# An encoder layer on one core: the first projections from an x that comes transposed, the norm as side work, the recurrences moved behind the first attention heads

## The chip, the cores and the metric

The kernel runs on one core of one Trainium2 chip. The metric is the device time of one execution in microseconds (us), as the median of the runs; lower is better. The engines are named as in the profile: PE is TensorE, DVE VectorE, ACT ScalarE, POOL GpSimd, SP SyncE. Each takes its own instructions in a fixed order, and an instruction that waits holds up all behind it on its engine.

## The reference

One layer with S = 256 tokens of D = 1024. The normed x goes through one wide matrix, whose columns feed four mixers; their outputs are gated, projected and added, and a feed-forward part and a gated embedding follow.

```python
xn = _rms_norm(x, norm1_g[i])
(a_x, a_g, b_q, b_k, b_v, c_q, c_kv, c_kpe,
 d_q, d_k, d_v, d_g, gate_logits) = jnp.split(xn @ w_in[i], IN_OFFSETS, axis=-1)
y_a = _rglru_mixer(a_x, a_g, conv_w[i], conv_b[i], lru_wa[i], lru_ba[i], lru_wx[i], lru_bx[i],
                   lru_lambda[i])
...
y_b = _diff_attention(b_q, b_k, b_v, diff_q_g[i], diff_k_g[i], diff_lam[i], diff_sub_g[i],
                      lam_init, cos_b, sin_b)
y_c = _mla(c_q, c_kv, c_kpe, mla_qa_g[i], mla_wuq[i], mla_kva_g[i], mla_wukv[i],
           mla_q_g[i], mla_k_g[i], cos_c, sin_c)
y_d = _retention(d_q, d_k, d_v, d_g, ret_gn_g[i], cos_d, sin_d)
gates = jax.nn.sigmoid(gate_logits.reshape(b, s, N_BRANCH, D_MODEL) + gate_b[i])
...
x = x + merged @ w_out[i]
h = _rms_norm(x, norm2_g[i])
x = x + jnp.square(jax.nn.relu(h @ w_ff1[i])) @ w_ff2[i]
ple_gate = jax.nn.sigmoid(_rms_norm(x, norm3_g[i]) @ w_ple_gate[i])
x = x + ple_gate * (p[i] @ w_ple_proj[i])
```

`_rglru_mixer` is a convolution over tokens, two gated linear recurrences (one in each direction) and a gelu gate; the other three are kinds of attention. The norm multiplies each token by one factor (over its 1024 values) and each column by a gain. A token's factor is the same for all columns, so it can be applied to a projection's rows afterwards as well.

## The kernel before, in words

**Weights.** All matrices are packed in one array in the order of their use. `load` (L364) brings up to 512 rows by 512 columns, 1 MB, into one of three `raw` buffers, by a DMA on SP's queue; an issue for a buffer that is not free waits, and so do the DMAs behind it. `pieces` (L374) turns 1024 columns of `raw` into two reduced-precision tiles: `hi`, a rounded copy (by ACT, or by DVE for every second piece from the eighth), and `lo`, the difference, always by DVE. There are five buffers for each (`NR`). The activations are split in the same way (`xTh`, `xTl`, by `split_scaled`, L223), and a product is three matmuls: hi with high, lo with high, hi with low. All of them go through the helper line L199.

**Two shapes of projection.** `a_mode` (L396) has the tokens in the output's rows: per 128 rows of weights six matmuls of 512 columns, into two PSUM banks. `b_mode` (L434) has the output's columns in rows: 48 matmuls of 256 columns per 256 columns of weights, into one bank. There are four such banks ("acc") and four for all else ("mm").

**Side work.** The element-wise parts are Python generators in the list `side`. After each load's worth of matmuls `tick` (L339) lets the first four of the list go on by a step each until a credit is used up; `finish` (L352) runs one to its end. A scheduler then sets the order of the instructions of each engine by priorities (`high_priority`): the pieces stand 60 instructions ahead of their place.

**The start.** x comes in rows (four DMAs, L231), then the column parameters (L232); ACT squares and sums x, DVE scales it by the tokens' factors (L457), 16 PE transposes and eight `split_scaled` give `xTh`, `xTl`. Then:

- four times `a_in(u)` (L506): a `b_mode` projection and a convolution (`xc`); each starts `a_mix(u)`: loads `bd` (block-diagonal gate matrices, L525), matmuls of `xc` with `bd`, sigmoids, exp, tanh, square and square root, then two scans on DVE, one per direction;
- `b_in(c)` for c = 0, 1: q, k, v of four heads each (`a_mode`), with side work `b_rot` (norm per head, rotation, transposes) and `b_mix` (scores, softmax);
- four times `a_out(u)` (L563), which finishes `a_mix(u)`, projects the gate, takes its gelu (`gel`) and multiplies; then `c_in` (the latents; 384 and 320 columns), the gates and the merges.

ACT keeps its functions in tables, and an ACT_TABLE_LOAD stands in its order where the next function is in another one: the sigmoids, the exponentials and tanh, the square roots and the gelu are in different ones here.

## Time and profile before

| | |
|---|---|
| median of 3 runs | 734.09 us (733.2 to 734.31) |
| the profiled execution | 732.92 us |
| its span, first to last instruction | 731.1 us |
| PE busy | 714.7 us, 98% of the span |
| DVE busy | 526.2 us, 72% |
| ACT busy | 427.7 us, 58% |
| POOL busy | 49.3 us, 7% |
| first instruction of PE | 7.51 us after the span's start |
| DMA | 128.47 MB, mean 176 GB/s |

The times of the trace count from the span's start. A group's row gives its source line, engine, operation, output and inputs, shapes and count, then its busy time, the mean duration of one in ns, and the idle time of the engine ahead of it with what ended it. Matmuls start closer together than they last (0.12 us apart at 0.28 us each, for 256 columns), so PE's pace is read from the starts. A full-precision (f32) matmul shows as two records.

### The profile page before, as it was taken

How to read it: one execution, taken by the hardware profiler on the slowest of the kernel's cores; microseconds unless marked ns; L12 is line 12 of the kernel's file. 1: busy time of each engine (PE TensorE's matmuls, PEld its weight loads, DVE VectorE, ACT ScalarE, POOL GpSimd, SP SyncE). 2: the span in 40 equal slices, each digit the busy share in tenths (PEclk: the TensorE clock that was granted, in tenths of full speed). 3: DMA queues.
4: the chain of work that ended last, by engine and by line, in shares of the span. 5: the costliest groups of instructions: out<-in, count | busy, mean ns of one | idle time of the engine just before them, and what ended most of it. 6: DMA issues, size and time to landing. Idle time of an engine off the chain costs nothing.

```text
span 731.1 us, 10616 instructions
## 1 busy us (share of the span) xinstructions
PE 714.7 (98%) x4066; PEld 622.6 (85%) x4066; DVE 526.2 (72%) x893; ACT 427.7 (58%) x744; POOL 49.3 (7%) x58
## 2 busy tenths in 40 slices
PE   5999999999999999999999999999999999999997
PEld 4988889997888898888888888878899999888886
DVE  5988978998777879976775788576666666446652
ACT  7589867483755996556654443545755555445551
POOL 0000012222011033110000101000000000000000
PEclk9999999999999999999999999999999999999999
DMA  8754544365344254444545475553565555636611
GB/s 312 260 212 173 172 173 145 114 248 182 134 162 137 91 177 169 173 159 144 179 166 217 138 256 197 191 184 143 177 225 176 173 177 185 215 118 229 233 53 58
DMA packets 22802, 128.47 MB, mean 176 GB/s; under 512 B 2656, under 2 KB 2912, under 8 KB 9440
## 3 DMA queue, kind: packets, MB, share of 16 engines
q1 hardware_dynamic: 22752, 127.80, 49.8%
q8 instruction: 32, 0.52, 0.3%
q14 instruction: 18, 0.15, 0.1%
HBM read 126.74 MB, written 1.05 MB: 175 GB/s over the span
## 4 chain that ended last, share of the span: by engine, by line
PE 64%; DVE 1%; ACT 0%; issue 0%
PE acc L199 57%; PE mm L199 3%; PE mm L212 2%; PE mm L203 1%; ACT hi L196 0%; DVE lo L190 0%; DVE gate L193 0%; DVE pg L190 0%; DVE y L193 0%; DVE xs L190 0%; ACT pg L196 0%
## 5 line engine op out<-in xcount | busy, mean ns | idle before, releaser
L190 DVE TENSOR_TENSOR lo<-raw,hi 128x1024 fp32r<-128x1024 f32 (+3 forms) x226 | 268.2, 1192 | 116.6 <-ACT hi L196 116.0
L196 ACT ACTIVATE hi<-raw 128x1024 fp32r<-128x1024 f32 (+2 forms) x200 | 207.7, 1043 | 192.6 <-PE acc L199 161.2
L199 PE MATMUL acc<-hi,xTh 128*128 128x512 f32 (+3 forms) x376 | 146.3, 389 | 0.0
L199 PE MATMUL acc<-hi,xTl 128*128 128x512 f32 (+3 forms) x376 | 142.8, 380 | 0.0
L199 PE MATMUL acc<-lo,xTh 128*128 128x512 f32 (+3 forms) x376 | 142.5, 379 | 0.0
L199 PE MATMUL acc<-hi,y 128*128 128x512 f32 x448 | 142.1, 393 | 0.0
L199 PE MATMUL acc<-xTl,hi 128*128 128x256 f32 x384 | 109.2, 285 | 0.2 <-DVE xTl L193 0.2
L199 PE MATMUL acc<-xTh,hi 128*128 128x256 f32 x384 | 109.2, 286 | 0.0
L199 PE MATMUL acc<-xTh,lo 128*128 128x256 f32 x384 | 108.7, 284 | 0.0
L199 PEld LDWEIGHTS acc<-hi,y 128*128 128x128 f32 x448 | 84.1, 188 | 17.5
L199 PE MATMUL acc<-lo,y 128*128 128x512 f32 x224 | 87.8, 392 | 0.0
L199 PEld LDWEIGHTS acc<-hi,xTl 128*128 128x128 f32 x376 | 70.6, 188 | 13.2
L199 PEld LDWEIGHTS acc<-hi,xTh 128*128 128x128 f32 x376 | 70.7, 188 | 12.9
L199 PEld LDWEIGHTS acc<-lo,xTh 128*128 128x128 f32 x376 | 70.8, 188 | 12.2
L199 PEld LDWEIGHTS acc<-xTl,hi 128*128 128x128 f32 x384 | 74.1, 193 | 0.7 <-DVE xTl L193 0.6
L199 PEld LDWEIGHTS acc<-xTh,hi 128*128 128x128 f32 x384 | 73.9, 193 | 0.1
L199 PEld LDWEIGHTS acc<-xTh,lo 128*128 128x128 f32 x384 | 73.8, 193 | 0.1
L199 PEld LDWEIGHTS acc<-lo,y 128*128 128x128 f32 x224 | 42.1, 188 | 8.3
L199 PE MATMUL acc<-hi,h 128*128 128x512 f32 x128 | 40.8, 398 | 0.0
L199 PEld LDWEIGHTS acc<-hi,h 128*128 128x128 f32 x128 | 24.0, 188 | 5.7
L199 PE MATMUL acc<-lo,h 128*128 128x512 f32 x64 | 25.3, 396 | 0.0
L199 PE MATMUL acc<-hi,cT 128*128 128x384 f32 (+1 forms) x80 | 24.2, 369 | 0.8 <-ACT cqp L196 0.8
(225 smaller groups left out, 889.9 us busy)
## 6 DMA issues: line engine op xcount, KB each, us to landing
raw<-in_weights_dram SPq DMA_DIRECT2D x104, 1024.0 KB, 4.8
raw<-in_weights_dram SPq DMA_DIRECT2D x6, 512.0 KB, 3.5
raw<-in_weights_dram SPq DMA_DIRECT2D x4, 576.0 KB, 3.8
bd<-in_lru_dram SPq DMA_DIRECT2D x8, 256.0 KB, 5.3
gb<-in_gate_b_dram SPq DMA_DIRECT2D x8, 256.0 KB, 5.2
dec<-in_decay_dram SPq DMA_DIRECT2D x8, 256.0 KB, 6.2
raw<-in_weights_dram SPq DMA_DIRECT2D x2, 768.0 KB, 4.3
raw<-in_weights_dram SPq DMA_DIRECT2D x2, 640.0 KB, 3.7
```

The lines of the kernel that those rows point to most:

```text
L190: nc.vector.tensor_tensor(out=o, in0=x, in1=y, op=op)
L196: nc.scalar.activation(o, x, f, **kw)
L199: nc.tensor.matmul(o, lhsT=lhsT, rhs=rhs, start=start, stop=stop)
L203: nc.tensor.matmul(o, lhsT=lhsT, rhs=rhs, start=start, stop=stop, skip_group_check=True)
L212: nc.tensor.transpose(o, x, ident[:x.shape[0], :x.shape[0]])
```

## The change

The inputs have a further array, `xT`, which is x with its columns in rows. The first projections are now q, k and v of heads 0 to 3, with x without the tokens' factors: `x1` is `xT` times the gain, split in hi and lo. The evacuations of these projections multiply by the factors `r1`, which `norm1`, a side generator, works out meanwhile from x in rows. `norm1` also makes the derived parameters, spreads the factors along columns by two matmuls, multiplies `xT` by them on POOL (`x1r`), and splits that into `xTh`, `xTl` for all later projections; the transposes are gone. The first weights come in three parts on SP's queue, between those of `xT`; the column parameters come on ACT's queue. The first four pieces have 512 columns in place of 1024, and the first two of their `hi` are DVE's. Twelve matmuls of zeros (`cold`) stand first on PE. The four `a_in` follow, and each `a_mix` is put ahead of the attention's generators in `side`.

```diff
+    raw0 = raws.tile([P, 2048], F32, tag="raw", name="raw", bufs=3)
     with tc.high_priority(FIRST):
-        for t in range(2):
-            for c in range(2):
-                w = slice(512 * c, 512 * c + 512)
-                nc.sync.dma_start(xs[:, t, w], a['x'][0, t * P:(t + 1) * P, w])
-        nc.sync.dma_start(par[:, :O_LATE], a['params'][:, :O_LATE])
+        nc.scalar.dma_start(par[:, :8], a['params'][:, :8])
+        nc.scalar.dma_start(par[:, 8:O_LATE], a['params'][:, 8:O_LATE])
+
+        cold = small.tile([P, P], F32, tag="cold", name="cold", bufs=1)
+        nc.vector.memset(cold, 0.0)
+        pt = mm_bank()
+        for _ in range(WARM):
+            mm(pt[:, 0:P], cold, cold, True, True)
...
-            if count[0] % 2 == 0 and count[0] in V_HI:
+            if count[0] <= 2 or count[0] % 2 == 0 and count[0] - 2 in V_HI:
...
-            for p0 in range(0, kc, 2):
-                kp = min(2, kc - p0)
+            fine = 1 if count[0] < 4 else 2
+            for p0 in range(0, kc, fine):
+                kp = min(fine, kc - p0)
...
-        with tc.high_priority(FIRST):
-            for t in range(2):
-                r_ = rstd(xs[:, t, :], lambda: SH("xsq"))
-                nc.vector.tensor_scalar(out=xs[:, t, :], in0=xs[:, t, :], scalar1=r_, scalar2=None, op0=MULT)
-            for k2 in range(4):
...
-                        transpose(pt[:, k, t * P:(t + 1) * P], xs[:, t, kk * P:(kk + 1) * P])
...
+        def norm1():
+
             for t in range(2):
+                for c in range(2):
+                    w = slice(512 * c, 512 * c + 512)
+                    nc.sync.dma_start(xs[:, t, w], a['x'][0, t * P:(t + 1) * P, w])
+            nc.sync.dma_start(par[:, O_LATE:], a['params'][:, O_LATE:])
+            yield 2.0
+            for t in range(2):
+                r1.append(rstd(xs[:, t, :], lambda: SH("xsq"), 'rst1'))
+                yield 1.5
+            derived_params()
+            yield 3.0
+
+            pt = mm_bank()[:, :S]
+            for t in range(2):
+                mm(pt[:, t * P:(t + 1) * P], r1[t].to_broadcast([P, P]), ident, True, True)
+            rows = SH("rows")[:, :S]
+            act(rows, pt, AF.Copy)
+            yield 0.5
+            for j in range(2):
+                nc.gpsimd.tensor_tensor(out=x1r[j], in0=x1r[j], in1=rows.unsqueeze(1).to_broadcast([P, 4, S]), op=MULT)
+                yield 0.3
+            for k in range(8):
+                split_scaled(xTh[:, k, :], xTl[:, k, :], x1r[k // 4][:, k % 4, :], c1('norm1_g', k))
...
+                if pre is not None:
+                    while len(r1) < 2:
+                        next(pre)
+                kw = [{} if pre is None else dict(scale=r1[t]) for t in range(2)]
...
-                        act(x[:, t, :], ps[t][:, 256 * p:256 * p + 256], AF.Copy)
+                        act(z[:, t, :], ps[t][:, 256 * p:256 * p + 256], AF.Copy, **kw[t])
...
+            nc.sync.dma_start(x1r[0][:, 0:2], a['xT'][:, 0:2])
+            nc.sync.dma_start(raw0[:, 0:512], src[:, 0:512])
+            nc.sync.dma_start(raw0[:, 512:1024], src[:, 512:1024])
+            nc.sync.dma_start(x1r[0][:, 2:4], a['xT'][:, 2:4])
+            nc.sync.dma_start(raw0[:, 1024:2048], src[:, 1024:2048])
+            nc.sync.dma_start(x1r[1], a['xT'][:, 4:8])
...
+        pre = start(norm1())
+        for p, (r0, qT, rq, rk, kT, _, v) in enumerate(b_in(0, (x1k(0), x1k(1)), pre)):
+            gb.append(start(b_mix(p, qT, rq, kT, v, yb), (r0, rk)))
+        finish(pre)
         for u in range(4):
             xc = a_in(u)
-            if u == 0:
-                derived_params()
             ha.append(L("rr").rearrange("p (f s) -> p f s", s=S))
             ga.append(start(a_mix(u, xc, ha[u])))
-        yb = yhl()
-        for c in range(2):
-            for p, (r0, qT, rq, r1, kT, _, v) in enumerate(b_in(c)):
-                gb.append(start(b_mix(2 * c + p, qT, rq, kT, v, yb), (r0, r1)))
+
+            side.insert(u, side.pop())
+        for p, (r0, qT, rq, rk, kT, _, v) in enumerate(b_in(1)):
+            gb.append(start(b_mix(2 + p, qT, rq, kT, v, yb), (r0, rk)))
```

**Where the instructions move.** First, ACT's first work before; `xsq` are the squares of x, `nst` the sums and factors.

```order
L196 ACT_TABLE_LOAD
L196 ACTIVATE eps<-eps 128x1
L196 ACTIVATE xsq,nst<-xs 128x512 x3
L196 ACTIVATE nst<-nst,eps 128x1
L196 ACTIVATE xsq,nst<-xs 128x512
L196 ACTIVATE nst<-nst,eps 128x1
L196 ACTIVATE xTh<-mm,par 128x256
L196 ACTIVATE hi<-raw 128x1024
```

And in the change, from the third row on; the y tiles at the top hold x1 and xT.

```order
L199 ACTIVATE y_119<-y_123,par 128x256 x4
L199 ACTIVATE hi<-raw 128x512 x2
L199 ACTIVATE y_121<-y_124,par 128x256 x4
L199 ACTIVATE hi<-raw 128x1024 x4
L199 ACTIVATE xsq,nst<-xs 128x512 x4
L199 ACTIVATE nst<-nst,eps 128x1 x2
L199 ACTIVATE bx<-acc,nst 128x256 x4
L199 ACTIVATE spt<-par 128x16
L199 ACT_TABLE_LOAD
L199 ACTIVATE spt<-spt 128x16
L199 ACTIVATE lams<-lams 128x2
L199 ACTIVATE hi<-raw 128x1024
```

The squares, the factors, the first evacuations (`bx`) and the start of the derived parameters now stand between the hi of the eighth piece and that of the ninth.

Second, SP's queue ahead of the bd matrices of the second recurrence (u = 1; bd_409 and bd_411), before:

```order
L371 DMA raw_424<-in_weights_dram 128x2048
L371 DMA raw_524<-in_weights_dram 128x2048
L371 DMA raw_594<-in_weights_dram 128x2048
L371 DMA raw_660<-in_weights_dram 128x2048
L525 DMA bd_409<-in_lru_dram 128x512
L525 DMA bd_411<-in_lru_dram 128x512
```

And in the change, where they are bd_728 and bd_730:

```order
L379 DMA raw_757<-in_weights_dram 128x2048
L379 DMA raw_853<-in_weights_dram 128x2048
L379 DMA raw_923<-in_weights_dram 128x2048
L379 DMA raw_989<-in_weights_dram 128x2048
L379 DMA raw_1036<-in_weights_dram 128x2048
L551 DMA bd_728<-in_lru_dram 128x512
L551 DMA bd_730<-in_lru_dram 128x512
```

raw_757 is the fourth recurrence projection's load, raw_853 and raw_923 are those of q in `b_in(1)`, raw_989 and raw_1036 those of k. PE uses bd_728 directly behind the fourth recurrence projection:

```order
L202 MATMUL acc_756<-xTh_114,lo_788 128x256
L202 MATMUL mm_817<-xc_476,bd_627 128x256 x2
L202 MATMUL mm_822<-xc_476,bd_627 128x256 x2
L202 MATMUL mm_828<-xc_565,bd_728 128x256 x2
L202 MATMUL mm_833<-xc_565,bd_728 128x256 x2
L202 MATMUL acc_851<-hi_855,xTh_114 128x512
L202 MATMUL acc_851<-lo_856,xTh_114 128x512
```

raw_1036 takes the buffer of raw_853, which is free when lo of its second piece (piece 24, lo_872) is made.

Third, ACT from the first gelu of `a_out` on, before:

```order
L196 ACT_TABLE_LOAD
L196 ACTIVATE gel<-acc 128x512
L196 ACTIVATE y_1181<-gel 128x512
L196 ACTIVATE hi<-raw 128x768
L196 ACTIVATE gel<-acc 128x512
L196 ACTIVATE y_1181<-gel 128x512
L196 ACTIVATE bsq<-bx 128x512
L196 ACTIVATE hi<-raw 128x768
```

And in the change, from the same gelu; the row ahead of these is the last of four sigmoids that read the matmuls with bd_919:

```order
L199 ACT_TABLE_LOAD
L199 ACTIVATE gel<-acc 128x512
L199 ACT_TABLE_LOAD
L199 ACTIVATE aa<-rr,sp 128x256
L199 ACTIVATE y_1183<-gel 128x512
L199 ACTIVATE rr<-rr,sp 128x256
L199 ACTIVATE aa<-rr,sp 128x256
L199 ACTIVATE hi<-raw 128x768
L199 ACTIVATE rr<-rr,sp 128x256
L199 ACTIVATE sq<-aa 128x512
L199 ACT_TABLE_LOAD
L199 ACTIVATE gel<-acc 128x512
```

The next hi of 768 columns (the third piece of `c_in`) stands 24 rows further down, behind five more table loads, four sigmoids, the third gelu and the last square roots. `aa` and `rr` are the recurrences' exponentials and tanh. DVE's way to the lo of that piece in the change, from the last squares on:

```order
L196 SCALAR_TENSOR_TENSOR rr<-sq,rr 128x512
L582 MEMSET aa 128x2
L687 TENSOR_REDUCE bsm<-mm 128x2 x2
L193 TENSOR_TENSOR bsm<-bsm,brs 128x2
L193 TENSOR_TENSOR ii<-ii,rr 128x512 x2
L586 SCALAR_TENSOR_TENSOR rr<-aa,ii 128x512 x2
L653 TENSOR_REDUCE brs<-bsq 128x8
L193 TENSOR_TENSOR rr<-rr 128x512
L193 TENSOR_TENSOR lo<-raw,hi 128x768
```

Row six (L586) is two scans. Over the whole program ACT has 24 table loads in its order, 18 before.

More of the change, by code (lines that the diff above doesn't have):

```diff
@@ L28 @@
 V_HI = range(8, 60)
+WARM = 12
 O_AX, O_AG, O_BQ, O_BK, O_BV = 0, 1024, 2048, 3072, 4096
@@ L160, in _pack @@
     import numpy as np
-    return {'x': np.asarray(w['x']), 'weights': _pack_weights(w), 'params': _pack_params(w), 'lru': _pack_lru(w),
+    return {'x': np.asarray(w['x']),
+            'xT': np.ascontiguousarray(np.asarray(w['x'])[0].T.reshape(8, P, S).transpose(1, 0, 2)), 'weights': _pack_weights(w), 'params': _pack_params(w), 'lru': _pack_lru(w),
             'pT': np.ascontiguousarray(np.asarray(w['p'])[0, 0].T.reshape(2, P, S).transpose(1, 0, 2)),
@@ L238, in encoder_kernel @@
         nc.vector.memset(eps[:, j:j + 1], v)
-    act(eps[:, 2:3], eps[:, 0:1], AF.Sqrt)
     nhalf = const.tile([P, 16], F32, name="nhalf")
@@ L255, in derived_params @@
     def derived_params():
-        nc.sync.dma_start(par[:, O_LATE:], a['params'][:, O_LATE:])
         gr = par[:, O_GR:O_LAM].rearrange("p (j c w) -> p j c w", j=2, c=2)
@@ L303, in encoder_kernel, with rstd @@
     xTl = near.tile([P, 8, S], F32R, name="xTl")
-    def rstd(src, scratch):
-        st = small.tile([P, 2], F32, tag="nst", name="nst")
+    def rstd(src, scratch, tag="nst"):
+        st = small.tile([P, 2], F32, tag=tag, name="nst", bufs=4 if tag == "nst" else 2)
         sq = scratch()
@@ L452, in SH @@
             return br.tile([P, 512], F32, tag="SH", name=name, bufs=NS)
-        with tc.high_priority(FIRST):
+        r1 = []
+        done = set()
+        def norm1():
             for t in range(2):
-                r_ = rstd(xs[:, t, :], lambda: SH("xsq"))
-                nc.vector.tensor_scalar(out=xs[:, t, :], in0=xs[:, t, :], scalar1=r_, scalar2=None, op0=MULT)
-            for k2 in range(4):
-                pt = mm_bank().rearrange("p (k s) -> p k s", s=S)
-                for t in range(2):
-                    for k in range(2):
-                        kk = 2 * k2 + k
-                        transpose(pt[:, k, t * P:(t + 1) * P], xs[:, t, kk * P:(kk + 1) * P])
-                for k in range(2):
-                    kk = 2 * k2 + k
-                    split_scaled(xTh[:, kk, :], xTl[:, kk, :], pt[:, k, :], c1('norm1_g', kk))
+                for c in range(2):
[19 more added lines that the diff above has]
+                split_scaled(xTh[:, k, :], xTl[:, k, :], x1r[k // 4][:, k % 4, :], c1('norm1_g', k))
+                if k % 2:
+                    yield 1.0
         def y4():
@@ L613, in b_in @@
                         ss = small.tile([P, 2, 4], F32, tag="brs", name="brs", bufs=8)
-                        pairs[p] += [start(b_rot(j, x, dst, ss)), dst, ss]
+                        pairs[p] += [start(b_rot(j, z, dst, ss), () if pre is None else (pre,)), dst, ss]
                     else:
-                        pairs[p].append(x)
+                        pairs[p].append(z)
             return pairs
@@ L945, in encoder_kernel, with x1k, get @@
         ha, ga, gb, gc = [], [], [], []
+        x1 = yhl()
+        early[W_in, 0, O_BQ] = raw0
+        x1r = [y4().bitcast(F32) for _ in range(2)]
+        with tc.high_priority(FIRST):
+            o = offs[W_in, 0, O_BQ][0]
+            src = a['weights'][o:o + 512 * 512].rearrange("(p c) -> p c", c=2048)
+            nc.sync.dma_start(x1r[0][:, 0:2], a['xT'][:, 0:2])
[4 more added lines that the diff above has]
+            nc.sync.dma_start(x1r[1], a['xT'][:, 4:8])
+            act(eps[:, 2:3], eps[:, 0:1], AF.Sqrt)
+        def x1k(i):
+            def get(k):
+                if k not in done:
+                    done.add(k)
+                    with tc.high_priority(FIRST if k == 0 else AHEAD_S + 20):
+                        split_scaled(x1[k // 4][0][:, k % 4, :], x1[k // 4][1][:, k % 4, :], x1r[k // 4][:, k % 4, :],
+                                     c1('norm1_g', k))
+                return x1[k // 4][i][:, k % 4, :]
+            return get
+        yb = yhl()
+        pre = start(norm1())
+        for p, (r0, qT, rq, rk, kT, _, v) in enumerate(b_in(0, (x1k(0), x1k(1)), pre)):
+            gb.append(start(b_mix(p, qT, rq, kT, v, yb), (r0, rk)))
+        finish(pre)
         for u in range(4):
             xc = a_in(u)
-            if u == 0:
-                derived_params()
             ha.append(L("rr").rearrange("p (f s) -> p f s", s=S))
             ga.append(start(a_mix(u, xc, ha[u])))
-        yb = yhl()
-        for c in range(2):
-            for p, (r0, qT, rq, r1, kT, _, v) in enumerate(b_in(c)):
-                gb.append(start(b_mix(2 * c + p, qT, rq, kT, v, yb), (r0, r1)))
+            side.insert(u, side.pop())
+        for p, (r0, qT, rq, rk, kT, _, v) in enumerate(b_in(1)):
+            gb.append(start(b_mix(2 + p, qT, rq, kT, v, yb), (r0, rk)))
         pace[0] = G1
```

9 lines of the change are left out of this document (6 added, 3 removed).

## The prediction

> **What bounds the kernel now.** I read the page first, then the waits of TensorE.
>
> ```profile
> PE 714.7 (98%) x4066; PEld 622.6 (85%) x4066; DVE 526.2 (72%) x893; ACT 427.7 (58%) x744; POOL 49.3 (7%) x58
> ...
> bd<-in_lru_dram SPq DMA_DIRECT2D x8, 256.0 KB, 5.3
> ```
>
> ```profile
> PE mm L212 <- DVE nst L190: 7.5, 1, 7.5
> ```
>
> TensorE (PE) is busy for 98% of the span; of its 16.4 us without work 7.5 lie ahead of its first instruction. So a change is worth what it does to the start, less what it makes PE wait for later. The timeline of PE shows that the start costs more than those 7.5 us.
>
> ```profile
> 7.51 0.66 PE L212 MATMUL mm<-ident,xs 128*128 128x128 f32 x2 [7.51 <-DVE nst L190]
> ...
> 11.74 0.56 PE L199 MATMUL acc<-xTh,hi 128*128 128x256 f32 x1
> ...
> 13.32 0.41 PE L199 MATMUL acc<-xTh,hi 128*128 128x256 f32 x1
> 13.54 0.35 PE L199 MATMUL acc<-xTl,hi 128*128 128x256 f32 x1
> ...
> 16.73 0.28 PE L199 MATMUL acc<-xTl,hi 128*128 128x256 f32 x1
> 16.85 0.28 PE L199 MATMUL acc<-xTh,lo 128*128 128x256 f32 x1
> ```
>
> ```profile
> 30.77 1.89 PE L199 MATMUL mm<-xc,bd 128*128 128x256 f32 x8
> ```
>
> ```profile
> 45.59 0.39 PE L199 MATMUL acc<-hi,xTl 128*128 128x512 f32 x1
> 45.82 0.39 PE L199 MATMUL acc<-hi,xTh 128*128 128x512 f32 x1
> ```
>
> The first column is the start, the second the duration. Starts lie 0.22 us apart at 13.3, while PE is fresh from its idle, and 0.12 us later on (256 columns; 0.23 for 512). At 30.77 the 144 matmuls of the first three recurrence projections are issued; at 0.12 us they are worth 17.3, so PE stands as if it had begun at 13.5 and never stopped. I call that its paid-up start; the wait for the first norm, the transposes, slow matmuls and short waits for xTl are all in it. If the changed kernel's matmuls can be dated in the same way, the difference of the two dates is the gain, and no single wait need be guessed.
>
> **The start, part by part.** Landings come from what DMA moved, ended waits on ACT, and costs from the groups of DVE and ACT:
>
> ```profile
> 0.00:5.00 5.00, 0.00 (x0) 0.00 (x0) 0.14 (x3) 2.78 (x6) 0.68 (x6) 1.00 0.59 179
> 5.00:10.00 5.00, 1.82 (x8) 1.45 (x9) 2.19 (x8) 2.47 (x10) 0.00 (x0) 1.00 1.02 386
> 10.00:15.00 5.00, 4.84 (x25) 4.55 (x24) 4.47 (x9) 5.00 (x11) 0.00 (x0) 1.00 1.01 418
> ```
>
> ```profile
> 3.67 0.63 ACT L196 ACTIVATE xsq<-xs 128x512 f32<-128x512 f32 x1 [1.46 <-DMA xs<-in_x_dram]
> ...
> 4.42 0.63 ACT L196 ACTIVATE xsq<-xs 128x512 f32<-128x512 f32 x1
> ```
>
> ```profile
> L190 DVE TENSOR_TENSOR lo<-raw,hi 128x1024 fp32r<-128x1024 f32 x210 | 255.4, 1221 | 116.5 <-ACT hi L196 116.0
> L384 DVE CAST hi<-raw 128x1024 fp32r<-128x1024 f32 x22 | 15.0, 684 | 0.6 <-PE acc L199 0.5
> ...
> L560 DVE TENSOR_TENSOR_SCAN rr<-aa,ii 128x512 f32<-128x512 f32 x8 | 9.7, 1218 | 0.1
> ...
> L190 DVE TENSOR_TENSOR lo<-raw,hi 128x768 fp32r<-128x768 f32 x8 | 7.6, 948 | 0.0
> L193 DVE SCALAR_TENSOR_TENSOR xc<-acc,par,xc 128x255 f32<-128x255 f32 x16 | 7.6, 473 | 0.1
> ...
> L190 DVE TENSOR_TENSOR ii<-ii,rr 128x512 f32<-128x512 f32 x8 | 5.5, 685 | 0.4 <-ACT rr L196 0.4
> ...
> L193 DVE SCALAR_TENSOR_TENSOR xTl<-mm,par,xTh 128x256 fp32r<-128x256 f32 x8 | 3.5, 479 | 1.3 <-ACT xTh L196 1.3
> ```
>
> ```profile
> L196 ACT ACTIVATE hi<-raw 128x1024 fp32r<-128x1024 f32 x188 | 199.3, 1063 | 188.3 <-PE acc L199 156.9 <-issue 26.4 <-DMA raw<-in_weights_dram 2.9
> L196 ACT ACT_TABLE_LOAD x18 | 23.1, 1283 | 2.9 <-DVE bsm L190 1.9 <-PEq L1087 0.7
> ...
> L196 ACT ACTIVATE aa<-rr,sp 128x256 f32<-128x256 f32 x16 | 7.3, 502 | 0.0
> ...
> L196 ACT ACTIVATE ii<-mm,par 128x256 f32<-128x256 f32 x16 | 6.8, 488 | 0.0
> ...
> L196 ACT ACTIVATE rr<-rr,eps 128x512 f32<-128x512 f32 x8 | 5.7, 728 | 0.0
> L196 ACT ACTIVATE bT<-mm,par 128x512 fp32r<-128x512 f32 x8 | 5.4, 679 | 0.0
> ...
> L196 ACT ACTIVATE gel<-acc 128x512 f32<-128x512 f32 x4 | 2.4, 588 | 0.0
> ```
>
> The last columns of a window are the clock, the DMA share and GB/s; those of a group are its busy time, the mean ns of one, and its idle time. A copied hi and its lo I call a piece, and number the pieces from the start. DMA had moved 0.9 MB by 5 us, 2.8 by 10 and 4.9 by 15, and the first 0.26 MB of before ended ACT's wait at 3.67. I read the landings of the new order off this sum and add 0.4 for completion: first x columns 3.6, first quarter of the weights 4.6, second load of weights (3.15 MB) 11.2, third 13.7, x in rows (5.24 MB) 16.2. That x in rows and the late parameters now stand on SP's queue behind the loads of three weight tiles delays only the squares, since no matmul needs them; the column parameters on ACT's own queue are issued before its table load, in time that it had free until 3.67. DVE paces the first pieces: two casts and los of 512 (0.36 and 0.61, half the 1024 rows), four x los (0.42 as they follow each other), two los, four x los: 4.6 + 2.0 + 1.7 + 1.2 + 1.7 = 11.2. Piece 5 waits for its load, its copy ends at 12.2, its lo at 13.4. PE then has ten matmuls of that piece and twelve of piece 6: 13.4 + 22 x 0.23 = 18.4. That is 48 matmuls, 10.9 us of work: paid-up start 7.5. The removed 16 transposes are in the 13.5 already. The 12 warm matmuls run from about 1 us in PE's empty time; full price each is half of a 256-column one of the block-diagonal kind, some 0.2 us, twice that when slow, so 2.4 to 4.8 us, over before 7. If they left PE slow, its matmuls would lag by 0.1 to 0.2 us each until about 12, mostly under DVE's pace: at most 1.5, and that is in the lower end below.
>
> Piece 9 is the next to be late. ACT copies 7 and 8 (to 15.6), takes four squares (spacing 0.75, to 18.7), two roots, four scaled evacuations (to 21.2), an absolute value, a table load (1.28), two exponentials (to 23.1) and then copies 9, to 24.1; its lo ends at 25.2. PE wants it at 18.4 + 5.5 = 23.9 and does the two broadcast matmuls meanwhile. Paid-up start 8.4: **gain 5.1** (6.5 if the squares run earlier between loads, 3.0 if landings come 1 us later and the warm-up fails). The evacuations with a token factor cost what the plain ones cost; the two 512-wide casts that go from ACT to DVE are in the walk.
>
> The normed copy xTh, xTl is needed only at the first projection of the recurrence, at 8.4 + 144 x 0.23 = 41.2. The factors' row is on ACT at 25.5; POOL then multiplies twice, and ACT, which takes its instructions in order, has the first five xTh ahead of the hi of piece 13. No row has such a multiply. The bounds are 1.2, DVE's row of 1024, and 4.9, four times that, the spread of POOL's own rows of one shape:
>
> ```profile
> L295 POOL TENSOR_SCALAR crk<-crk 128x4 f32<-128x4 f32 x4 | 4.8, 1206 | 0.3
> ...
> L295 POOL TENSOR_SCALAR bss<-bss 128x4 f32<-128x4 f32 x4 | 1.2, 291 | 52.1 <-DVE bss L190 52.1
> ```
>
> I take 2.4, near the lower end, since nothing else is queued on POOL there: products at 28.0 and 30.4, hi 13 at 32, hi 15 at 35, and on DVE lo 16 at 37.4 and the last xTl at 41.2. PE wants piece 13 at 36 and xTl from 41.2 on, one each 0.36 us: nothing late at 2.4, some 2 us at 4.9.
>
> **The block-diagonal weights.** The first load bd of recurrence 1 now stands on SP's queue behind the load raw_1036, which needs a buffer that is free only after the lo of piece 24. Before:
>
> ```profile
> 15.89 13.76 SPq L371 DMA_DIRECT2D raw<-in_weights_dram  x4
> 29.70 0.91 SPq L525 DMA_DIRECT2D bd<-in_lru_dram  x2
> ```
>
> Issued at 29.7 and 5.3 us to land: 35, and PE used it only after its 38.2. In the new order PE comes to it at 41 + 17.3 + 1.6 + 1.6 + 5.8 + 1.6 = 69 (recurrence projections from 41). DVE, from 41.2, has ahead of lo 24: eight los, four casts, four reductions, twelve xc, fourteen rope and scale steps; 24.5 us by the means, 22 with the 0.1 by which they follow earlier. So the buffer is free at 63.2 to 65.7, bd is issued half a us later and lands at 69 to 71.5. PE would wait 0 to 2.5 us, with b_in(1) queued behind the wait. I take **1.0**.
>
> **The latent projection.** After the second-last group of block-diagonal matmuls (bd_919), ACT has, in its order up to the last two square roots: eight sigmoids, 12 exponentials and tanh, three gelu, three copies of y, three squares, three roots, two bT, one hi, and eight table loads. By the means: 8 x 0.49 + 12 x 0.50 + 3 x 0.73 + 11 between 0.59 and 0.68 + 0.8 + 8 x 1.283 = 30.1. Two rows show how closely they follow:
>
> ```profile
> 108.88 0.91 ACT L196 ACTIVATE aa<-rr,sp 128x256 f32<-128x256 f32 x2
> 109.69 0.89 ACT L196 ACTIVATE rr<-rr,sp 128x256 f32<-128x256 f32 x2
> ```
>
> Two take 0.81, so 35 of them save 3.5: 26.6. Behind the roots DVE has two products (0.69), two scans (1.22), a reduction and a sum, and only then the lo of the third piece of c_in (0.95): 5.5 to 6.1. Ready 32.1 to 36.2 after bd_919. PE's cover from there: 96 + 48 matmuls of a_out at 0.12 (17.3), four block-diagonal ones (1.6), eight transposes (1.6), 24 of 384 columns at 0.17 (4.1), 24 score matmuls (2.9) = 27.5. All of this is counted from one event, so an earlier or later start doesn't change it. A wait of 4.6 to 8.7; the fourth piece, five DVE steps later, adds 1.5. **Cost 7.0**, bounds 3.5 and 9.5. PE is then behind by that much for good: what follows it, the latent vectors and the gates, hangs on the same pieces. Before, the recurrences were over by then, and the gelus shared one table load; that cover is what the later place of the recurrences takes away.
>
> Behind the latent projection PE has nearly the rows that it had; I count that at 0. Sum: -5.1 + 1.0 + 7.0 = **+2.9**. The profiled execution (732.92, span 731.1) would become 735.8; the median of the three runs lies 1.17 above it, so I predict 734.09 + 2.9 = 737.0.
>
> **Rivals.** A measurement of this kernel can tell about 0.2%, 1.5 us, from no change.
> - Faster: ACT and DVE keep ahead, since the page has ACT at 58%. Then both later waits vanish and 734.1 - 5.1 = 729.0 is left. It decides if ACT's stretch is under 21 us, 6 less than counted. Against it: its eight table loads alone are 10.3. 0.20.
> - No difference: the c_in wait is at its lower end, 3.5, and bd costs 1.0: 733.5; it is so if the wait is under 5.6. Range 732.6 to 735.5. 0.18.
> - POOL and DVE hold each other up. For it: POOL's rows of one shape, 0.29 and 1.21, as if one sometimes waited for DVE. Multiplies of 4.9 between DVE's los make pieces 10 to 13 late by about 3: 740.0. 0.07. The Trainium skill (SBUF — State Buffer, Who interferes with whom) says that a DVE instruction with two SBUF inputs and a GpSimd instruction that reads SBUF block each other fully; by that rule DVE's los would stand still for both multiplies, and this rival would hold; no long pair of the kind is in this trace.
> - The forecast, 0.55: by its own bounds 735.5 to 741.5.
>
> The range takes in most of the faster case: 730.5 to 741.5. Faster 0.20, same 0.18, slower 0.62.
>
> **What would show it.** In the trace after: first main matmul near 5, b_in(0) without a wait over 2 us after 14; PE waiting up to 2.5 us at the eight block-diagonal matmuls after the fourth projection; 4 us or more on lo of the 768-wide pieces, with ACT full through the a_out stage and 24 table loads in place of 18. If PE doesn't wait for those pieces, the forecast is wrong on its largest term; if the matmuls up to piece 9 are through before 22 or after 28, on its first.

## The result and the profile after

The changed kernel takes 742.27 us (median), the kernel before, run beside it on the same chip, 733.86. One of its four executions was slow (890.57 at a granted clock of 0.752); the other three have a median of 741.92, and from these come the ratio of 1.0108 (95% interval 1.0094 to 1.0122) and all differences below, while the expectations count from 742.3. So the change costs 8.1 us. The prediction had 737.0 with 730.5 to 741.5: right in direction, but outside at the upper end, by 0.8 (by 0.4 for the three). The profiled execution took 741.92 with a span of 740.1, 9.0 more than the 731.1 before; the profiled execution before was itself 0.9 below that median of 733.86, hence 9.0 here and 8.1 in the medians.

The page's row of busy times, and the waits of TensorE (us in total, times, longest):

```profile
PE 720.8 (97%) x4078; PEld 626.6 (85%) x4078; DVE 534.3 (72%) x904; ACT 440.9 (60%) x759; POOL 57.2 (8%) x60
```

```profile
PE acc L202 <- ACT hi L199: 4.9, 2, 3.9
PE acc L202 <- DVE lo L193: 4.8, 3, 2.8
PE mm L202 <- DMA bd<-in_lru_dram: 1.1, 1, 1.1
```

The 7.5 us for the first norm are gone, and new waits for hi and lo have come. **The start**, in PE's timeline:

```profile
6.31 0.68 PE L202 MATMUL acc<-hi,y 128*128 128x512 f32 x1
...
14.45 0.73 PE L202 MATMUL acc<-hi,y 128*128 128x512 f32 x2 [0.98 <-ACT hi L199]
...
15.71 0.50 PE L202 MATMUL acc<-lo,y 128*128 128x512 f32 x1 [0.53 <-DVE lo L193]
...
34.05 0.50 PE L202 MATMUL acc<-lo,y 128*128 128x512 f32 x1 [1.47 <-DVE lo L193]
...
44.88 0.28 PE L202 MATMUL acc<-xTh,hi 128*128 128x256 f32 x1
```

At 44.88 the 144 matmuls of 512 columns are issued; at 0.23 they are worth 33.1, so the paid-up start is 11.8, against 13.5 before: a gain of 1.7. Two rows, of DVE and of ACT, show that the start was late from its first landings on: DVE's first cast stands behind small steps on the column parameters, which came at 5.62, and the hi of piece 5 waits for its load until 13.34.

```profile
5.62 0.15 DVE L275 TENSOR_SCALAR gng<-par 128x1 f32<-128x1 f32 x1 [4.60 <-DMA par<-in_params_dram]
...
13.34 2.01 ACT L199 ACTIVATE hi<-raw 128x1024 fp32r<-128x1024 f32 x2 [0.83 <-DMA raw<-in_weights_dram]
```

The row at 34.05 is the longest of the waits of the start, and the timelines of POOL and of DVE show what made that lo (of piece 12) late:

```profile
27.84 5.00 POOL L487 TENSOR_TENSOR y<-y,rows 128x1024 f32<-128x1024 f32 x2 [26.55 <-ACT rows L199]
```

```profile
25.16 0.18 DVE L193 TENSOR_TENSOR spt<-spt 128x16 f32<-128x16 f32 x1
...
28.13 2.37 DVE L193 TENSOR_TENSOR spt<-spt 128x16 f32<-128x16 f32 x1
...
30.53 2.34 DVE L288 TENSOR_SCALAR spt<-spt 128x16 f32<-128x16 f32 x1
```

Sixteen elements take 0.18 us at 25.16 and 2.37 us beside POOL's first multiply, 2.34 beside its second: for 4.7 us DVE did next to nothing. The Trainium skill (SBUF — State Buffer, Who interferes with whom) has a full block between GpSimd and a DVE instruction with two SBUF inputs; the first pair agrees.

**The block-diagonal weights**, then **the latent projection**, in PE's timeline:

```profile
73.48 1.97 PE L202 MATMUL mm<-xc,bd 128*128 128x256 f32 x8 [1.09 <-DMA bd<-in_lru_dram]
```

```profile
144.81 1.70 PE L202 MATMUL mm<-bT 64*128 64x256 f32 x24
150.39 1.01 PE L202 MATMUL acc<-hi,xTh 128*128 128x384 f32 x2 [3.87 <-ACT hi L199]
154.15 0.69 PE L202 MATMUL acc<-lo,xTh 128*128 128x384 f32 x1 [2.76 <-DVE lo L193]
154.64 0.52 PE L202 MATMUL acc<-hi,xTl 128*128 128x384 f32 x1
154.96 0.52 PE L202 MATMUL acc<-hi,xTh 128*128 128x384 f32 x1
```

The two waits make 6.6 us, and behind them the matmuls start 0.32 apart; ahead of the waits, at 144, it was 0.17. The stretches show why (PE, its loads, DVE, ACT and POOL with counts, then the clock, the DMA share and GB/s):

```profile
140.00:145.00 5.00, 5.00 (x33) 4.75 (x33) 2.50 (x5) 4.99 (x10) 0.00 (x0) 1.00 0.00 0
145.00:150.00 5.00, 1.51 (x24) 1.31 (x23) 3.52 (x10) 4.97 (x9) 0.00 (x0) 1.00 0.00 0
150.00:155.00 5.00, 1.85 (x5) 1.35 (x6) 5.00 (x7) 4.67 (x7) 2.19 (x2) 0.51 0.00 0
155.00:160.00 5.00, 5.00 (x18) 5.00 (x17) 5.00 (x13) 3.52 (x9) 2.64 (x3) 0.50 0.20 33
160.00:165.00 5.00, 5.00 (x35) 4.83 (x33) 4.54 (x13) 4.13 (x13) 0.00 (x0) 0.96 1.00 390
```

ACT is full from 140 to 150, and PE stands for most of the second half of that: the first wait is for ACT's queue. In the second wait DVE is full (5.00 of the 5 us from 150): there it is DVE's queue, the products, scans and reductions behind the last roots. The granted clock is 0.5 from the end of the first wait until about 160. Half of the 5.0 busy us from 155 to 160, of some 0.9 ahead of it and 4% of the five behind it make 3.1 us. The Trainium skill (TensorE: Matmul & The Clock Gate, Part 1) has the clock halved after an idle window of some 3.4 us; the wait of 3.87 agrees.

The sum: -1.7 (start) + 1.1 (bd) + 6.6 (waits) + 3.1 (half pace) = +9.1, against a span longer by 9.0. Nothing else of size is left, as far as the sum can tell. How much of the 3.1 is a cost of its own, and what fills ACT's queue, was left to experiments.

### The profile page after: what moved, and what is told of

Same layout as the page of the kernel before. It is cut to its first block, busy times and chain, and to the rows that moved or that the text cites. A ratio compares the mean times of both kernels' runs of the same rounds, so it can differ in the third digit from the quotient of the medians.

```text
span 740.1 us, 10680 instructions
## 1 busy us (share of the span) xinstructions
PE 720.8 (97%) x4078; PEld 626.6 (85%) x4078; DVE 534.3 (72%) x904; ACT 440.9 (60%) x759; POOL 57.2 (8%) x60
## 4 chain that ended last, share of the span: by engine, by line
PE 63%; DVE 1%; ACT 0%; issue 0%
PE acc L202 57%; PE mm L202 3%; PE mm L215 2%; PE mm L206 1%; ACT hi L199 0%; DVE lo L193 0%; DVE gate L196 0%; DVE pg L193 0%; DVE y L196 0%; DVE xs L193 0%; ACT pg L199 0%
## 5 line engine op out<-in xcount | busy, mean ns | idle before, releaser
L193 DVE TENSOR_TENSOR lo<-raw,hi 128x1024 fp32r<-128x1024 f32 (+4 forms) x228 | 267.7, 1183 | 119.6 <-ACT hi L199 118.7
L199 ACT ACTIVATE hi<-raw 128x1024 fp32r<-128x1024 f32 (+3 forms) x200 | 206.4, 1037 | 187.2 <-PE acc L202 156.5
L202 PE MATMUL acc<-hi,y 128*128 128x512 f32 x544 | 173.1, 393 | 1.7 <-ACT hi L199 1.0
L202 PE MATMUL acc<-hi,xTh 128*128 128x512 f32 (+3 forms) x328 | 127.8, 392 | 3.9 <-ACT hi L199 3.9
L202 PE MATMUL acc<-lo,xTh 128*128 128x512 f32 (+3 forms) x328 | 125.2, 382 | 2.8 <-DVE lo L193 2.8
L202 PE MATMUL acc<-hi,xTl 128*128 128x512 f32 (+3 forms) x328 | 125.2, 382 | 0.0
L202 PEld LDWEIGHTS acc<-hi,y 128*128 128x128 f32 x544 | 102.2, 188 | 23.6 <-ACT hi L199 1.4
L202 PE MATMUL acc<-lo,y 128*128 128x512 f32 x272 | 106.8, 393 | 2.0 <-DVE lo L193 2.0
L202 PEld LDWEIGHTS acc<-lo,xTh 128*128 128x128 f32 x328 | 62.7, 191 | 13.6 <-DVE lo L193 3.3
L202 PEld LDWEIGHTS acc<-hi,xTl 128*128 128x128 f32 x328 | 62.5, 191 | 11.3
L202 PEld LDWEIGHTS acc<-lo,y 128*128 128x128 f32 x272 | 51.1, 188 | 13.4 <-DVE lo L193 3.2
```

Source lines behind the costliest of these rows:

```text
L193: nc.vector.tensor_tensor(out=o, in0=x, in1=y, op=op)
L199: nc.scalar.activation(o, x, f, **kw)
L202: nc.tensor.matmul(o, lhsT=lhsT, rhs=rhs, start=start, stop=stop)
```

## The experiments

Each ratio is to the kernel before, run beside it, with its 95% interval.

**The order alone.** The kernel before keeps its start, and only the sequence changes:

```
+...
+for ... in enumerate(b_in(0)): ...
 for u in range(4):
     xc = a_in(u)
     ...
     ga.append(start(a_mix(u, xc, ha[u])))
+    side.insert(u, side.pop())
-for c in range(2):
-    for ... in enumerate(b_in(c)): ...
+for ... in enumerate(b_in(1)): ...
```

> The kernel before with its old start (x in rows, squares, sixteen transposes) and the changed order alone: the first four heads' q, k, v, then the four recurrences' projections, then the other four heads, each recurrence's side work put ahead of the attention's. Theory A (the later place of the recurrences costs the time: 1.1 us at the block-diagonal weights, 6.6 us of waits in the latent projection, and about 3 us of matmuls at half pace behind those waits): 733.9 + 10 = about 744, with waits of 5 us or more on hi and lo of the 768-wide pieces and a granted clock near 0.5 just behind them. Theory B (the new start lost the time, the order is harmless): 733 to 735, and no wait over 2 us at the latent projection.

Measured 753.08, 1.0259 [1.0245, 1.0273]. The groups of ACT and PE's waits from 120 to 175:

```profile
L196 ACT ACT_TABLE_LOAD x29 | 37.2, 1283 | 1.2 <-PEq L1088 0.7
```

```profile
PE mm L199 <- ACT baT L196: 5.3, 1, 5.3
PE mm L199 <- ACT be L196: 5.0, 1, 5.0
```

The order costs, by some 19 us instead of the 10 expected: with the old start, PE stands in the same stretch, but at matmuls of the attention that need ACT's results, and not at the pieces that theory A named; at the latent vectors it waits for 3.8, against 1.4 before. So theory B falls, and of theory A only its first half is shown, that the order costs the time. ACT's table loads are 29, against 24 in the changed kernel and 18 before.

**The recurrences' side work not first**: the line `side.insert(u, side.pop())` is left out of the changed kernel.

> The changed kernel without the line that puts the recurrences' side work ahead of the attention's, one part of the change undone. If the recurrences' place in the list is what keeps the gelu projections supplied, without it they are worked off in a burst ahead of each gelu projection, TensorE waits there, and it is slower: 746 or more. Rival (theory E alone, the number of table loads decides: the program has two fewer): 739 to 740.

Measured 769.39, 1.0478 [1.0465, 1.0492], with 23 loads. PE's waits from 120 to 175:

```profile
PE mm L202 <- ACT rr L199: 6.4, 1, 6.4
PE acc L202 <- ACT hi L199: 4.8, 1, 4.8
PE acc L202 <- DVE lo L193: 1.8, 1, 1.8
PE mm L202 <- DVE y L196: 1.2, 1, 1.2
```

That line is no part of the loss; it saves 27 us of what the later place would otherwise cost. The rival falls too: with one table load less than the changed kernel this is the slowest of all.

**The start.** First the warm-up (`WARM = 0`), then the multiplies on DVE:

```
-nc.gpsimd.tensor_tensor(out=x1r[j], in0=x1r[j], ...)
+nc.vector.tensor_tensor(out=x1r[j], in0=x1r[j], ...)
```

> The changed kernel without the twelve warm matmuls. If they are what lets TensorE run at full pace from its first main matmul: slow matmuls (0.34 apart and more) from 6.3 on, the paid-up start up to 1.5 us later, 742.3 to 743.8. Rival (VectorE's pieces set the pace of the start, or the clock comes up by itself before the long stretch): 742.3, no difference.

> The changed kernel with the two multiplies by the tokens' factors (128 x 1024 each) on VectorE instead of GpSimd. Theory D (GpSimd's multiplies hold VectorE up for 5 us, TensorE loses 1.7 us at 34 by that): VectorE spends about 2.4 us more in place of the 4.6 us in which it stood, the small operations beside it take 0.2 us instead of 2.3, the wait at 34 goes: 742.3 - 1.7 = 740.6. Rival (the pieces at 34 are late for lack of VectorE's time, whoever multiplies): 742 to 743.

Without the warm-up 741.49, 1.0106 [1.0093, 1.0120]: no difference to the changed kernel. PE's timeline there:

```profile
11.28 0.86 PE L202 MATMUL acc<-hi,y 128*128 128x512 f32 x2
11.98 0.40 PE L202 MATMUL acc<-lo,y 128*128 128x512 f32 x1
12.22 0.63 PE L202 MATMUL acc<-hi,y 128*128 128x512 f32 x2
...
15.98 0.50 PE L202 MATMUL acc<-lo,y 128*128 128x512 f32 x1 [0.16 <-DVE lo L193]
```

Matmuls are 0.43 apart up to the first of these rows (11.28) and 0.23 from 12 on, so the warm-up did speed the first ones; but the next piece is late in both kernels, and the time saved was waited for there, 0.98 and 0.53 in the changed kernel against 0.16 here. The rival holds.

With the multiplies on DVE 738.63, 1.0069 [1.0055, 1.0083]: 3.3 less (3.6 in the spans), more than the 1.7 expected. DVE's timeline, and the first recurrence matmul in PE's:

```profile
28.12 0.17 DVE L193 TENSOR_TENSOR spt<-spt 128x16 f32<-128x16 f32 x1
...
28.29 1.22 DVE L487 TENSOR_TENSOR y<-y,rows 128x1024 f32<-128x1024 f32 x1
...
31.69 0.17 DVE L288 TENSOR_SCALAR spt<-spt 128x16 f32<-128x16 f32 x1
...
43.10 0.28 PE L202 MATMUL acc<-xTh,hi 128*128 128x256 f32 x1
```

The same small steps take 0.17 again, DVE multiplies in 1.22 where POOL took 2.5, and the wait at 34 is gone. So is the wait for bd: SP issues it at 62.0 instead of 68.4, as it would if DVE's earlier los free the buffer for the load that stands ahead of it. The first recurrence matmul comes 1.8 earlier (43.10 for 44.88); 1.8 + 1.1 make 2.9 of the 3.6. The latent projection's waits stay (3.8 and 3.7).

**The half clock.** Matmuls of zeros, added to the latent projection's own accumulator, fill the waits, so that PE is not idle; first one place, then both:

```
+if name == W_in and n0 == O_CQ and k0 == 4:
+    for _ in range(16):                        # 22, and 12 more between hi and lo
+        mm(ps[0][:, 0:P], cold, cold, False, False)
```

> The changed kernel with 16 more matmuls (128 by 128, float32, of zeros, added to the latent projection's own accumulator, so that the sums are unchanged), put at the place where TensorE waits for the third piece of that projection. They take about 3.7 us at full clock and fill the first wait only. Theory C (the idle time makes TensorE run at half pace for some 6 us afterwards, and that costs about 3 us of its own): the granted clock stays at 1.0 from 150 to 162, and the time is 742.3 - 3 = 739.3. Rival (the pieces behind the wait are late anyway, so the slow matmuls cost nothing): 742, with other waits in place of the slow matmuls.

> As the run with one filler, but with both waits of the latent projection's third piece filled: 22 matmuls of zeros ahead of its hi, 12 between its hi and its lo, again added to the projection's own accumulator. The first filler left gaps of 2.3 and 1.8 us, and the clock still fell. Theory C (the half-pace matmuls behind the waits cost about 3 us of their own): clock 1.0 from 145 to 165, time 742.3 - 3 = 739.3, if the fillers don't outlast the waits. Rival (ScalarE and VectorE set the pace there, and the slow matmuls only use up time in which TensorE would wait): 742, waits of the same sum as the slow matmuls before them.

One filler: 741.74, 1.0110 [1.0096, 1.0124]; both: 741.31, 1.0107 [1.0091, 1.0123]. With one, two gaps of 2.3 and 1.8 us were left, with 0.7 us of matmuls between them, and the clock fell all the same. With both it stayed (columns as above):

```profile
155.00:160.00 5.00, 5.00 (x32) 4.58 (x30) 5.00 (x14) 4.71 (x15) 2.38 (x2) 1.00 0.14 36
```

The matmuls from 156 to 160 stand 0.17 apart, but neither ratio differs from the changed kernel's 1.0108 by more than the noise (the medians fell by 0.2 and 0.6, not 3). The edit also moved ACT's order: a gelu now stood ahead of the hi, and PE used the lo at 155.7 instead of 154.15. From there to the first matmul of 320 columns PE takes 4.9 us with both fillers (155.68 to 160.61) and 7.1 in the changed kernel (154.15 to 161.22). So the slow matmuls are real, and no rival wait takes their place in that stretch, but what they cost in time these two runs don't show.

**What ACT's queue holds.** Tanh in place of the gelus (`AF.Gelu_apprx_tanh` to `AF.Tanh`; the gelu is left out), in the changed kernel, in the kernel before, and in the changed kernel with the multiplies on DVE:

> The changed kernel with tanh in place of the four gelus, so that ScalarE need not load a table for each gelu and one back (the gelu itself is left out, nothing else changes). Theory E (ScalarE's table loads between the recurrences' roots, exponentials and the gelus are what the new order adds: 24 loads against 18): 16 to 18 loads, some 8 us less on ScalarE between 118 and 153, the waits at the latent projection fall from 6.6 to under 2 and with them the slow matmuls: about 734. Rival F (the side work as a whole has lost its cover, table loads or not; what is freed here is waited for at the next place, as it was when the gates were put first): 739 to 742.

> The kernel before with tanh in place of its four gelus (the gelu is left out), as a control of the run that did this to the changed kernel. Theory E: there the gelus come one after another with one table load, beside other work, so nothing on the path goes: 732.5 to 734. Rival (tanh is worth 8 us for a reason of its own, not by the new order): 725 to 727.

> The changed kernel with both costs taken away at once: tanh in place of the gelus (the gelu is left out), multiplies on VectorE. Each alone gave -8.3 and -3.6. If they are separate places on TensorE's path (34 and 70 us there, 145 to 160 here), they add up: 742.3 - 8.3 - 3.6 = 730.4, and what is left against the kernel before with tanh (734.9) is the start's own gain, 4.5, near the 5.1 of the prediction. Rival (the multiplies' 3.6 is mostly a shift that the latent projection's wait then took up differently, so that the start itself gains little): 733 to 734.

Measured 733.96, 1.0005 [0.9997, 1.0014]; 734.91, 1.0020 [1.0010, 1.0030]; and 731.05, 0.9969 [0.9957, 0.9981]. ACT's loads in the changed kernel with tanh, and all that PE waits for from 120 to 175:

```profile
L199 ACT ACT_TABLE_LOAD x20 | 25.7, 1283 | 2.0 <-PEq L1146 1.6
```

```profile
PE acc L202 <- DVE lo L193: 1.7, 1, 1.7
```

Four loads fewer, 5.1 us, and 8.0 us are gone, while the kernel before gains nothing. So the interleaved gelus are what makes the pieces late. In the changed kernel with tanh the granted clock stays at 1.0 from 140 to 165; its waits are less by 4.9 (6.6 to 1.7), and the 3.1 put down to the half pace bring that to 8.0, the whole difference. That is the best sign here that the 3.1 are a cost of their own; it is a subtraction, and no run changes the clock alone. The third run adds the two up (8.0 + 3.3 = 11.3 against 10.9 measured); against the kernel before with tanh it is 3.9 faster. Its first recurrence matmul starts at 43.04, a paid-up start of 9.9, 3.6 before the old one. So the start's own gain is 3.6 to 3.9 when nothing disturbs it; what else the two kernels wait for (1.7 at the latent projection here, 2.0 for a transpose there) nearly cancels.

**Other places for the gelus.** First the gates ahead of the gelu projections; then, with the multiplies on DVE, the gelu projections behind the gates or directly behind the latent projection:

```
+gs = gates(0)
 for u in range(4): finish(ga[u]); a_out(u, ha[u], ya)
 cs = c_in()
 ...
-gs = gates(0)
 merge(True, gs, ya, 'w_br_a')
```

```
-for u in range(4): finish(ga[u]); a_out(u, ha[u], ya)
 cs = c_in()
 ...
 gs = gates(0)
+for u in range(4): finish(ga[u]); a_out(u, ha[u], ya)
 merge(True, gs, ya, 'w_br_a')
```

In the third kernel the loop stands one line higher, ahead of `gates(0)`.

> The changed kernel, but the gate projection (two column blocks of 512, some 22 us of TensorE work) is put between the fourth recurrence's q, k, v and the gelu projections, so that ScalarE and VectorE have longer for the recurrences' side work. Theory A (TensorE runs out of cover while ScalarE works off the recurrences): the waits in the latent projection and the slow matmuls behind them go, 742.3 - 6.6 - 3 = about 733, within 2 us. Theory B (the start lost the time): 741 to 743. Rival A2 (the side work is handed out by credit, and the tail of it only moves along with the gelu projections): a wait of 3 us or more stays, 738 to 742.

> The changed kernel with the multiplies on VectorE (738.6) and the order of the later projections changed: the latent projection directly after the last q, k, v, then the gate projection, and only then the four gelu projections and their merge. Theory E (the gelus between the recurrences' steps cost the table loads, the recurrences lack cover): when the gelus come, the recurrences are over, they share one table load, 18 loads in all, and no wait of over 2 us at the latent projection: 738.6 - 7.5 - 2 = 729 to 731. Rival F (what is freed is waited for at the latent vectors or the next projections): 737 to 739.

> As the run before it, but with the gelu projections directly behind the latent projection and the gates behind them: only 14 us of cover are added for the recurrences, the latent vectors keep the gates as cover. Theory E: most recurrences are over by the first gelu, about 20 loads, 731 to 734. Rival F: 737 to 739.

741.75, 1.0109 [1.0095, 1.0123]; 737.31, 1.0048 [1.0036, 1.0060]; 735.67, 1.0024 [1.0014, 1.0033]. In all three the waits for hi and lo at the latent projection are gone (0.2 is left in the third). With the gates first, PE's waits from 175 to 300 are these, 8.9 in all, where the changed kernel has 1.5:

```profile
PE acc L202 <- ACT cqp L199: 5.0, 3, 2.1
PE mm L215 <- DVE by L193: 1.9, 2, 1.1
PE mm L215 <- DVE bx L193: 1.3, 1, 1.3
PE acc L202 <- ACT cv L199: 0.7, 1, 0.7
```

So none of that run's three theories holds whole: the waits go, as A said, and the time stays, as B had it. What is freed is waited for elsewhere, as in the rival F of the runs with tanh: the rows are those of the latent's second projections and of the heads. The second kernel's time is within rival F's range, the third's between the theories; they have 23 and 24 loads, not the 18 and 20 expected.

**The gelus together.** The projections only copy their sums; the gelus come as one piece of side work, bound to the last recurrence by a zero bias taken from it (multiplies on DVE); then the pace between the fourth q, k, v and the second gates (G1) is 4.0 and 5.0 instead of 3.0, and 4.0 with G0 at 3.5:

```
-act(gel, ps, AF.Gelu_apprx_tanh)
-tt(gel, rr, gel, MULT)
-split(*yw(yy, 2 * u), gel)
+act(gel, ps, AF.Copy); gels.append(gel)
+def a_gel(yy):
+    zb = ...  # ha[3] * 0.0
+    for u in range(4): act(gels[u], gels[u], AF.Gelu_apprx_tanh, bias=zb)
+    yield 2.4
+    for u in range(4): tt(gels[u], ha[u], gels[u], MULT); split(...); yield 2.0
...
-    finish(ga[u])
...
+gel = start(a_gel(ya), tuple(ga))
+side.insert(0, side.pop())
 gs = gates(0)
+finish(gel)
```

> The changed kernel with the multiplies on VectorE (738.6) and the gelus taken out of the gelu projections: these only copy their sums to SBUF (four copies of 0.6 us more on ScalarE) and no longer wait for the recurrences; the four gelus come together as one piece of side work after the last recurrence, tied to it by a bias of zero taken from its result, while the gates are projected. Theory E (the table loads between gelus and recurrence steps, and the recurrences' lack of cover, make the waits at the latent projection): about 20 loads, no wait over 2 us at the latent projection, 738.6 - 8 = 730 to 732, faster than the kernel before. Rival F (what is freed is waited for at the latent vectors, the merge or the latent's second projections): 736 to 739.

> The kernel with the gelus together (736.9), with the pace of the side work between the fourth q, k, v and the second gates raised from 3.0 to 4.0. Theory G (the time that the gelus' place freed was lost because the attention's side work behind the recurrences is handed out too slowly, and then crowds the latent's second projections, where TensorE waits 7.6 us between 244 and 294): fewer waits there, 732 to 734. Rival (the crowding is ScalarE's and VectorE's total work, pace or not): 736 to 738.

> The same with the pace at 5.0. Theory G: no less good than pace 4, 730 to 733, until a wait ahead of the merge shows that the side work crowds the gates instead. Rival: 736 to 739.

> The same with 4.0 and with the first pace at 3.5 instead of 3.0, so that the recurrences too are handed out sooner, from the first projections on. Theory G: 731 to 733. Rival (VectorE is full from 40 to 80 and ScalarE from 80 to 120, so sooner means that a piece is late there): a new wait of some us between 60 and 120, 736 or more.

736.88, 1.0046 [1.0032, 1.0059]; 733.39, 1.0003 [0.9994, 1.0012]; 737.72, 1.0056 [1.0043, 1.0068]; 735.49, 1.0029 [1.0019, 1.0039]. In none is there a wait of over 0.7 us from 120 to 175. From 175 to 300 the first waits 8.4 in all, with pace 4 it is 6.8:

```profile
PE acc L202 <- ACT cqp L199: 4.7, 2, 4.4
PE mm L215 <- DVE by L193: 1.2, 1, 1.2
PE mm L215 <- DVE cT L196: 0.9, 1, 0.9
```

Pace 4 gives 3.5 us, inside theory G's range, though the waits that G names fell by only 1.6. Pace 5 takes the gain back, with fewer waits there still (4.5 in all), and is in its rival's range; more at the first pace lies between the two. So G is not shown: a better pace was found, and why it is better is open. The count of loads is not the measure either: the kernel with pace 4 has 24, as many as the changed kernel, and is 8.5 faster.

**The gelu worked out from tanh**, the whole reference computed (multiplies on DVE); then the sigmoids of the recurrences from tanh too:

```
-act(gel, ps, AF.Gelu_apprx_tanh)
-tt(gel, rr, gel, MULT)
+act(gel, ps, AF.Square)
+stt(gel, gel, 1 / 0.044715, ps, ADD, MULT)
+act(gel, gel, AF.Tanh, scale=0.044715 * (2 / pi) ** 0.5)
+stt(gel, gel, 1.0, ps, ADD, MULT)
+stt(gel, rr, 0.5, gel, MULT, MULT)
...
-act(dst[:, f, :], ps[:, f, :], AF.Sigmoid, bias=c1(bn, ...))
+act(dst[:, f, :], ps[:, f, :], AF.Tanh, scale=0.5, bias=bh[:, c:c + 1])
...
```

> The changed kernel with the multiplies on VectorE and the gelu worked out from tanh (a square and a tanh on ScalarE, two more steps on VectorE for each gelu: 2.4 us more on ScalarE and some 5.5 on VectorE in all than the run with tanh alone, 731.1), so the whole reference is computed and ScalarE loads no table for the gelus. Theory E: the loads cost the time, not the gelu's arithmetic: 731 to 733.5, at or under the kernel before. Rival (VectorE, which has the los of the late pieces behind these steps, passes their 5.5 us on to TensorE): 735 to 738.

> The kernel before this one with the recurrences' sigmoids worked out from tanh too (half scale and half bias into the tanh, the other half taken up by scales and biases that follow, no further instruction but one at the start), so that only the square roots need a table of their own: some 12 to 14 loads in all against 24, 8 to 9 us less on ScalarE than in the kernel before this one. Theory E: what is left of the waits at the latent projection goes, 730 to 731.5, faster than the kernel before the change. Rival (TensorE waits for nothing there any more, ScalarE's time is free): the same as the kernel before this one, within 0.7.

737.36, 1.0055 [1.0043, 1.0068], and 733.56, 1.0002 [0.9993, 1.0011]. PE's waits from 120 to 175 in the first, and ACT's loads in the second:

```profile
PE acc L202 <- DVE lo L193: 2.3, 2, 1.7
PE mm L202 <- DVE bT L196: 1.3, 1, 1.3
```

```profile
L199 ACT ACT_TABLE_LOAD x14 | 18.0, 1283 | 1.9 <-PEq L1152 1.6
```

The first has 21 loads, one more than the run with tanh alone and multiplies on DVE (731.05), and is 6.3 us slower than that. Of the 7.6 that tanh gave there (738.63 to 731.05) only 1.3 are left once each gelu has two more steps on DVE and one more on ACT; both waits end on DVE, and the rival's range holds. The second has seven loads less than the first, gains 3.8, and is level with the kernel before; its theory E and its rival both miss. So theory E is right that ACT's loads delay the pieces, and wrong that they alone do. Taken together, the runs say that PE waits for the whole queue of both engines ahead of the latent projection's pieces.

No kernel that computes the whole reference came out clear of the kernel before; the best two (pace 4 and the last one) are level with it. Where the start's gain goes in the last one is in its trace: a wait of 1.9 at the latent projection, and some 1.7 us of half pace behind it (the clock in the third column from the end):

```profile
151.00:152.00 1.00, 1.00 (x6) 1.00 (x6) 1.00 (x4) 0.85 (x4) 1.00 (x1) 0.56 0.00 0
152.00:153.00 1.00, 1.00 (x6) 1.00 (x5) 1.00 (x4) 1.00 (x4) 0.00 (x1) 0.50 0.00 0
```

With pace 4 there are the waits from 175 to 300 and a clock of 0.66 from 255 to 260, behind the longest of them (4.4). In that profiled execution (734.69, above the median of 733.39) the clock was 0.66 from 15 to 20 too, and the first recurrence matmul came at 44.67 instead of 43.10.

## Why the prediction was wrong

- **The start, "gain 5.1": the step that failed.** 1.7 was there. Undisturbed it is 3.6 to 3.9, inside the stated 3.0 to 6.5 but under the value taken. The first main matmul started at 6.31, not near 5, and piece 5 had its hi on PE at 14.45 and its lo at 15.71. The walk had the landings too early: it had the first weights at 4.6, while DVE came to its first cast only behind the parameters, at 5.75; it had the second load at 11.2, while ACT's copy waited for it until 13.34. Piece 9, which the walk had as late, was not waited for. (8.4 + 144 x 0.23 is 41.5, not 41.2; nothing hangs on it.)
- **"Nothing late at 2.4" for POOL's multiplies** failed, the larger part of that miss (1.8 of 3.4). The time of one was right (2.5), but it was put beside DVE's work, and DVE's steps stood still beside both multiplies. The rival in which the two hold each other up was real and had got 0.07; it named the pieces (10 to 13) and 740.0, since it put multiplies at 4.9. The prediction names the rule in that rival and leaves it out of its sum.
- **The block-diagonal weights, 1.0:** 1.1 measured, and that is luck. In the prediction's walk DVE doesn't stand still, and where it doesn't, in the run with the multiplies on DVE, there is no such wait.
- **The latent projection, 7.0:** 6.6 of waits, on the predicted piece, with 24 loads as predicted and ACT full. The longer wait was for its hi (3.9), and the lo took 2.8, not the 4 or more that was to show it; the score matmuls took 1.7, not 2.9, and the fourth piece wasn't waited for. The mechanism is right, and the run with tanh (-8.0) and its control show the cause.
- **Missing from the sum:** the half clock behind the waits, put at nothing without a reason. In the trace it is 3.1; the fillers leave its cost in time open, and the run with tanh leaves 3.1 for it by subtraction. The profile before has no long wait after its start, but its first matmuls, 0.22 apart instead of 0.12, showed what an idle PE does (its clock column reads 1.00 there and doesn't show it).
- **Warm-up:** it did what it should and gained nothing; counted at nothing, rightly, for pieces that DVE and the landings pace.
- **"Nothing behind the latent projection"** holds: from 175 on both kernels have nearly the same waits (2.4 and 3.5 us in all).

Sizes in the traces: -1.7 + 1.1 + 6.6 + 3.1, against -5.1 + 1.0 + 7.0. The start (3.4) and the clock (3.1) make up the difference of 6.2 to the forecast; the other two terms nearly cancel.

## What to carry to other kernels

Moving side work later costs what the engines that do it then queue ahead of the next operands, so walk that queue on both engines, table loads included, from the event at which both kernels stand alike. When a wait on TensorE comes to some 2 us or more, add the slow matmuls that may follow it to its price (here up to 3 us), and don't put a long GpSimd instruction beside VectorE's operand work as if it were free. Where a wait is taken away, look for the place where the same work comes up next before counting the gain.
